# A transformer block on one core: group A's y kept whole, the last pair projected by halves, a third buffer for probability pieces, and a root on GpSimd

## The chip, the cores and the metric

The kernel runs on one core of one Trainium2 chip, in float32 throughout its interface. The metric is device time in microseconds (us), the median of several runs; lower is better. The engines are called by these names: TensorE (PE in the profile, PEld for its weight loads), VectorE (DVE), ScalarE (ACT), GpSimd (POOL) and SyncE (SP), whose queue issues nearly all DMAs of this kernel.

## The reference

A block of a streaming encoder for 1024 tokens of width 1024, cut to what matters:

```python
n = rms_norm(x, norm1_g)
proj = n @ w_in                       # columns: qa 512, ka 128, va 128, qb 512, kb 512, vb 512
ya = mixer_a(qa, ka, va, sinks)       # 8 heads of 64, 2 key heads, window of 3 chunks of 64, ALiBi, sinks
yb = mixer_b(qb, kb, vb, rel_bias)    # 8 heads of 64, own chunk and 8 before it, a bias by clipped distance
y = concat(rms_norm(ya, out_norm_a_g), rms_norm(yb, out_norm_b_g))
h = x + y @ w_out
u = square(relu(rms_norm(h, norm2_g) @ w_ff1))   # 1024 -> 4096
h = h + u @ w_ff2                                # 4096 -> 1024
out = rms_norm(h, final_norm_g)
```

## The kernel before, in words

**Precision.** A float32 operand is split into a high part (rounded, written by ScalarE) and a low part (what is left, by VectorE or GpSimd), and a product is three matmuls, high x high, high x low and low x high (`mm3`, L193). So every operand of a product costs one ScalarE copy and one subtraction before TensorE may read it.

**Stages.** First the input is loaded, normalised and split into `nT[t][hl][g]` (L257): two halves of 512 tokens, high and low, four tiles each, 16 pages in all. A *page* (L94) is a tile of 4 KB for each partition; 35 of them (`NPAGES`) serve in turn for weights, projected q, k and v, y and the rest. Weights come through three *stages* (L97): `load_weight` (L209) loads 512 KB into a stage, and makes the high part on ScalarE (L223) and the low part on GpSimd in pieces of 256 columns (L228). Then group A's attention runs, then group B's, then the output projection and the two feed-forward products, which are TensorE from end to end.

**Attention.** Heads go in pairs, four of group A and four of group B. A unit of group B (`UnitB`, L754) is one head and one half of the queries, so a pair has four units. For each block of 128 queries it computes scores on TensorE, adds the bias and takes the minimum on VectorE (L570, L572), and the exponential on ScalarE (L573). `upper` (ScalarE, L805) and `lower` (VectorE, L810) turn two blocks of probabilities into float16 high and low pieces H (tag `P16`, two buffers), and a transposing DMA on SyncE's queue (L813) brings H to G, which the matmul `av` reads (`apply`, L823). The bias of one head lies in one of two tiles `bias_b`; it is loaded in two DMAs (L613, L614) that leave out two corners, which were set to a large negative value once (L532, L533). The bias of the next user of a tile is asked for at score 1 of the unit before (`next_bias`, L786).

**What fills TensorE meanwhile.** A queue of generators, the `Filler` (L901), is worked off in steps between the rows of attention: 16 steps, of three matmuls each, for every projection of k, q or v of a later pair (`in_proj`, L433), and at the end 64 steps of group A's share of the output projection, `op_A` (`out_proj_a`, L954). `ready(2)` (L911) runs the first piece of the first two generators of the queue, up to their first `yield`: that piece asks for weights, and for "out" it loads group A's y for the first 512 tokens (L888) and four output weights. So "out" is begun when the last v projection comes to the head of the queue.

```python
    def step(self):
        while self.queue:
            self.ready(2)
            try:
                next(self.queue[0][1])
                return
            except StopIteration:
                self.queue.pop(0)
```

TensorE's order is the program's, written out by hand (`pe`, L130). The other engines' and SyncE's orders are set by a scheduler when the kernel is built, from its own estimate of times; each engine then works strictly in that order, and so a waiting instruction holds up what is queued behind it.

**Group A's y.** When both heads of a pair have done a half of the tokens, `finish` (L625) squares Y for the group's norm (GpSimd, L659, L669, L670), splits Y into a page y by `split_y` (L850) and stores it, 512 KB, to `yd` in DRAM (L638). For pairs 0 and 1 the split applies the gain `ogc` (L854 on ScalarE, L857 on VectorE); pairs 2 and 3 (`PLAIN`) are split without a gain (L860 on ScalarE, two subtractions on GpSimd), and the gain is applied to the output weight instead, by an extra ScalarE pass over each half of the stage (L222). The norm's factor `rA` comes from `group_rstd` (L867): eight matmuls, and then an inverse root by four Newton steps of four small VectorE instructions (L878 to L881). It is read first where `op_A` is moved out of PSUM (L976). Group B's last pair keeps its y on the chip, in two pages `y7` named ahead (L989).

Of the kernel before, what the change touches and what calls it, by code (L numbers as in the profile page):

```python
# [17 lines left out]
P = 128  # L18
SEQ = 1024
D = 1024  # L20
# [10 lines left out]
WITH = ["", "", "k", "qv", "k", "qv", "k", "qv"]  # L31
NPAGES = 35
LOW_COLS = 256
# [10 lines left out]
POOL_NORM = ((1, 0), (1, 1))  # L44
PLAIN = (2, 3)
EARLY = 7
# [6 lines left out]
def kernel(  # L53
# [37 lines left out]
    def f(ap):  # L91
        return ap.bitcast(F32)
# [115 lines left out]

    def load_weight(src, shape, name, low_engine, cuts=1, pieces=1, gain=None):  # L209

        st = stage(shape, f"st_{name}")
        w = [page(shape, f"w{hl}_{name}") for hl in range(2)]
        key = "o" if name[0] == "o" else None

        def steps():
            n = shape[1] // cuts
            for i in range(0, shape[1], n):
                load(st[:, i : i + n], src[:, i : i + n])
                for j in range(i, i + n, n // pieces):
                    c = slice(j, j + n // pieces)  # L220
                    if gain is not None:
                        in_turn(key, nc.scalar.activation(st[:, c], st[:, c], AF.Copy, scale=gain))  # L222
                    in_turn(key, nc.scalar.activation(w[0][:, c], st[:, c], AF.Copy))  # L223
# [15 lines left out]

    yd = dram([8, P, 2, 2, HALF], "yd")  # L240
    hB = [dram([P, 2, D], f"hB{n}") for n in range(TB // 2)]
# [147 lines left out]
    def values_b(acc, name, dst, t):  # L389

        if t == 0:
            halves[name] = main.tile([P, 2, HALF], F32, tag="tst", bufs=2, name=f"ts_{name}")
        st = halves[name]
# [38 lines left out]

    def in_proj(c0, kind, name, dst, new):  # L433

        w = proj_weight(c0, name, nc.gpsimd)
        yield
        for t in range(2):
            acc = aps.tile([P, HALF], F32, tag="w", bufs=2, name=f"ip_{name}_{t}")
            for k in range(NK):
                project(acc, w, t, (k,))  # L440
                if k == NK - 1:
                    if t == 0 and new is not None:
                        dst.extend(new(name))
                    place(acc, kind, name, dst, t, nc.gpsimd)
                yield

    dve, pool = nc.vector, nc.gpsimd
# [82 lines left out]
    bias_b = [at.tile([P, 5 * P], F32, name=f"b_B{s}") for s in range(2)]  # L530
    for b in bias_b:
        nc.gpsimd.memset(b[:HD, 5 * P - HD :], NEG)  # L532
        nc.gpsimd.memset(b[HD:, :HD], NEG)  # L533

# [52 lines left out]
    class Pair:  # L587
# [7 lines left out]
        def biases(self):  # L595
            if self.kind == "A" and self.j == 0:
                return first_bias
            if self.bias:
                return self.bias
            for s in range(2):  # L600
                if self.kind == "B":
                    self.load_bias(s)
                    continue
                h = 2 * self.j + s
                b = atA.tile([P, 2 * P], F32, tag="bias", bufs=2, name=f"b_A{h}")
                nc.sync.dma_start(b, dist)
                nc.gpsimd.tensor_scalar(b, b, 2.0 ** -(h + 1), None, ALU.mult)
                self.bias.append(b)
            return self.bias

        def load_bias(self, s):
            b = bias_b[s]
            nc.sync.dma_start(b[:HD, : 5 * P - HD], relb[2 * self.j + s][:HD, : 5 * P - HD])  # L613
            nc.sync.dma_start(b[HD:, HD:], relb[2 * self.j + s][HD:, HD:])  # L614
# [7 lines left out]
        def gain(self):  # L622
            return self.V[2] if self.kind == "B" else None

        def finish(self, t):  # L625

            by_act = self.kind == "B" and self.m < 7
            if not by_act:
                self.squares(t, by_act)
            Y = self.out[t]  # L630
            if self.y is None:
                y = page([P, 2, HALF], f"y{t}_{self.m}")
                low = split_y(y, Y, self.m, by_act, self.gain())

                def rest():
                    if by_act:
                        low()
                    nc.sync.dma_start(yd[self.m, :, t], f(y))  # L638

                if by_act:  # L640
                    late.append(rest)
                else:
                    rest()
            else:
                split_y(self.y[t], Y, self.m, False, self.gain())
            if by_act:
                self.squares(t, by_act)
# [106 lines left out]
    class UnitB:  # L754
# [10 lines left out]
        def score(self, b):  # L765
# [20 lines left out]
        def next_bias(self):  # L786
# [3 lines left out]
            pairs_b[j].load_bias(s)  # L790

# [57 lines left out]

    def split_y(y, src, m, wait=False, gain=None):  # L850

        if m not in PLAIN:
            gain = ogc[:, m : m + 1] if gain is None else gain
            nc.scalar.activation(y[:, 0], src, AF.Copy, scale=gain)  # L854

            def low():
                return nc.vector.scalar_tensor_tensor(y[:, 1], src, gain, f(y[:, 0]), ALU.mult, ALU.subtract)  # L857

            return low if wait else low()
        nc.scalar.activation(y[:, 0], src, AF.Copy)  # L860
        for c in (slice(c, c + LOW_COLS) for c in range(0, HALF, LOW_COLS)):
            split_l(nc.gpsimd, y[:, 1, c], src[:, c], y[:, 0, c])

    def new_y(m):
        return [page([P, 2, HALF], f"y{t}_{m}") for t in range(2)]

    def group_rstd(kind, psum, tag, bufs, r):  # L867
# [9 lines left out]
        for _ in range(4):  # L877
            nc.vector.tensor_tensor(q, r, r, ALU.mult)  # L878
            nc.vector.tensor_tensor(q, q, v, ALU.mult)
            nc.vector.tensor_scalar(q, q, -0.5, 1.5, ALU.mult, ALU.add)  # L880
            nc.vector.tensor_tensor(r, r, q, ALU.mult)  # L881
        return r

    nc.vector.tensor_scalar(nsink, psink, -1.0, None, ALU.mult)
    def load_y(m, halves=range(2)):
        y = [page([P, 2, HALF], f"y{t}_{m}") for t in halves]
        for tile_y, t in zip(y, halves):
            nc.sync.dma_start(f(tile_y), yd[m, :, t])  # L888
        return y

    def out_weight(m):

        return load_weight(w_out[m * P : (m + 1) * P, :], [P, D], f"o{m}", pool, 1, 2, ogc[:, m : m + 1] if m in PLAIN else None)

# [6 lines left out]
    class Filler:  # L901
# [79 lines left out]
    fill = Filler()  # L981
    units = []
    fill.add("A1", ahead_A1, True)
    for j in range(4):
# [3 lines left out]
        units += [(UnitA(pair, i0), f"A{j}", A_FILL) for i0 in range(0, TB, 2)]  # L988
    y7 = new_y(7)  # L989
    for j in range(4):  # L990
        Q, K, V = [], [], []
        fill.add(f"B{j}", in_proj(KB0 + j * P, "k", f"kB{j}", K, new_k))
        fill.add(f"B{j}", in_proj(QB0 + j * P, "q", f"qB{j}", Q, new_q))
        fill.add(f"B{j}", in_proj(VB0 + j * P, "v", f"vB{j}", V, None))
        pair = Pair("B", j, Q, K, V, y7 if j == 3 else None)
# [598 lines left out]
```

## Time and profile before

| | |
|---|---|
| median of 3 runs | 1059.55 us (1058.63 to 1060.02) |
| the profiled execution | 1060.42 us |
| its span, first to last instruction | 1058.6 us |
| granted TensorE clock, mean of the span | 0.988 |
| busy: TensorE, VectorE, ScalarE, GpSimd | 1024.1, 690.4, 585.1, 420.7 us |
| group A's y: stores and loads of group A and B | 14 and 14, 512 KB each |
| DMA traffic | 187.71 MB, mean 177 GB/s |

In a line of the profile, "L165 PE MATMUL op_A<-w_o,y" is a matmul issued at line 165 (a helper) that writes tile op_A and reads w_o and y; buffer numbers are left out. In the timeline the first two columns are the start and the duration in us, and a bracket gives the idle time of the engine before the instruction and what released it. SPq is the issuing of DMAs by SyncE: its duration is that of the issue, not of the transfer. In the table of stretches each engine has its busy time and, in brackets, its count of instructions; PEclk is the share of the full clock that was granted to TensorE. In a group of instructions, three durations stand for the shortest, the median and the longest in ns.

### The profile page before, as it was taken

To read this page: it belongs to the slowest core of one execution; us is meant where nothing else is said; L and a number is where in the kernel's file an instruction comes from. 1 tells how busy PE (TensorE), PEld (TensorE's weight loads), DVE (VectorE), ACT (ScalarE), POOL (GpSimd) and SP (SyncE) were. 2 spreads that over 40 slices of the span, in tenths; PEclk is the share of its full clock that TensorE was granted. 3 is DMA by queue.
4 is the path that set the end of the run, shared out by engine and by line. 5 is a ranking of instruction groups with operands and counts; after the bars stand their busy time and mean duration, and the time that the engine had idled before them with its cause. 6 is when DMAs were issued, how large, how long until landed. Compare 5 with 4: busy or idle time off the path is not lost.

```text
span 1058.6 us, 13930 instructions
## 1 busy us (share of the span) xinstructions
PE 1024.1 (97%) x4803; PEld 832.7 (79%) x4803; DVE 690.4 (65%) x1075; ACT 585.1 (55%) x973; POOL 420.7 (40%) x307
## 2 busy tenths in 40 slices
PE   9999999979968899999999999999999999999997
PEld 7888887757746768888888888888888888888886
DVE  6577787858654725796434425436879877778667
ACT  8677767647664756675554454455533333333347
POOL 0566785322343373305554444345114024024025
PEclk9999999989989999999999999999999999999999
DMA  9954548899899993315534525417997535532004
GB/s 356 264 151 132 144 111 205 177 206 212 178 253 247 208 310 117 119 47 177 193 122 163 191 104 179 159 74 246 379 400 252 179 122 164 179 114 98 1 1 159
DMA packets 145222, 187.71 MB, mean 177 GB/s; under 512 B 78848, under 2 KB 96256, under 8 KB 145152
## 3 DMA queue, kind: packets, MB, share of 16 engines
q1 hardware_dynamic: 145008, 186.56, 58.4%
q8 instruction: 38, 0.62, 0.2%
q14 instruction: 32, 0.26, 0.1%
q10 hardware_dynamic: 144, 0.26, 0.1%
HBM read 105.00 MB, written 45.09 MB: 142 GB/s over the span
## 4 chain that ended last, share of the span: by engine, by line
PE 61%; DVE 2%; DMA 1%; ACT 1%; issue 0%; ACTq 0%; DVEq 0%
PE f L165 27%; PE f_a L165 16%; PE f_c L165 8%; PE op_B L165 4%; PE f_b L165 4%; DMA G_B<-H_B 1%; DVE X L171 1%; PE tp L168 0%; PE end L165 0%; PE op_A L165 0%; DVE S L1139 0%; DVE T L1168 0%; PE ss_B L165 0%; DVE H_B L810 0%; PE av_B L165 0%
## 5 line engine op out<-in xcount | busy, mean ns | idle before, releaser
L165 PE MATMUL f<-X,W 128*128 128x512 f32 x1344 | 305.9, 389 | 0.1
L165 PEld LDWEIGHTS f<-X,W 128*128 128x128 f32 x1344 | 252.0, 188 | 52.9 <-DVE X L171 0.5
L165 PE MATMUL f_a<-V,U 128*128 128x512 f32 x756 | 173.5, 389 | 0.0
L171 POOL TENSOR_TENSOR U<-u,U 128x1024 fp32r<-128x1024 f32 x32 | 79.7, 2492 | 227.5 <-PE f_c L165 135.8
L165 PEld LDWEIGHTS f_a<-V,U 128*128 128x128 f32 x756 | 141.8, 188 | 29.7 <-DVE C L1483 0.3
L171 POOL TENSOR_TENSOR W<-T,W 128x1024 fp32r<-128x1024 f32 x29 | 75.7, 2612 | 139.3 <-ACT W L1190 139.3
L165 PE MATMUL f_c<-V,U 128*128 128x512 f32 x384 | 88.4, 389 | 0.0
L165 PEld LDWEIGHTS f_c<-V,U 128*128 128x128 f32 x384 | 72.1, 188 | 15.0
L1190 ACT ACTIVATE V<-Z 128x1024 fp32r<-128x1024 f32 x32 | 33.9, 1059 | 88.3 <-PE f_a L165 44.6
L810 DVE SCALAR_TENSOR_TENSOR H_B<-P_B,rc_B,H_B 128x640 f16<-128x640 f32 (+2 forms) x64 | 52.8, 847 | 31.6 <-ACT H_B L805 31.3
L171 POOL TENSOR_TENSOR W<-w,W 128x1024 fp32r<-128x1024 f32 x23 | 57.2, 2490 | 32.1 <-ACT W L1190 32.0
L1190 ACT ACTIVATE V<-w 128x1024 fp32r<-128x1024 f32 x24 | 25.4, 1059 | 80.1 <-issue 34.3
L1239 DVE TENSOR_TENSOR k<-f,k 128x1024 f32<-128x1024 f32 x24 | 29.3, 1221 | 61.9 <-PE f L165 61.9
L171 DVE TENSOR_TENSOR V<-w,V 128x1024 fp32r<-128x1024 f32 x24 | 50.4, 2103 | 27.2 <-ACT V L1190 26.8
L573 ACT ACTIVATE P_B<-P_B,nm_B 128x640 f32<-128x640 f32 (+2 forms) x64 | 44.3, 692 | 42.7 <-DVE nm_B L570 22.0
L165 PE MATMUL op_A<-w_o,y 128*128 128x512 f32 x192 | 56.7, 426 | 8.7 <-ACT w_o L223 6.8
L1190 ACT ACTIVATE U<-u 128x1024 fp32r<-128x1024 f32 x56 | 58.5, 1045 | 11.4 <-DMA ud<-k 6.8
L165 PE MATMUL av_B<-G_B,VvB 128*128 128x128 f16 (+3 forms) x208 | 44.6, 302 | 13.5 <-DMA G_B<-H_B 13.5
L1233 ACT ACTIVATE k<-f 128x1024 f32<-128x1024 f32 x24 | 24.6, 1026 | 59.2 <-PE f L165 59.2
L805 ACT ACTIVATE H_B<-P_B,rc_B 128x640 f16<-128x640 f32 (+2 forms) x64 | 40.9, 686 | 22.8 <-DMA G_B<-H_B 12.1
L165 PE MATMUL ip_qB<-nT,w_qB 128*128 128x512 f32 x192 | 52.0, 405 | 1.1 <-DVE ts_kB L359 0.8
L165 PE MATMUL ip_kB<-nT,w_kB 128*128 128x512 f32 x192 | 52.6, 401 | 0.0
(245 smaller groups left out, 1934.5 us busy)
## 6 DMA issues: line engine op xcount, KB each, us to landing
w<-in_w_ff_dram SPq DMA_DIRECT2D x64, 512.0 KB, 4.9
u<-ud SPq DMA_DIRECT2D x56, 512.0 KB, 4.6
ud<-k SPq DMA_DIRECT2D x48, 512.0 KB, 3.2
KkB<-ts_kB SPq DMA_DIRECT2D x64, 128.0 KB, 2.3
yd<-y SPq DMA_DIRECT2D x14, 512.0 KB, 3.1
y<-yd SPq DMA_DIRECT2D x14, 512.0 KB, 7.3
xr<-in_x_dram SPq DMA_DIRECT2D x8, 512.0 KB, 8.7
QqB<-ts_qB SPq DMA_DIRECT2D x32, 128.0 KB, 2.9
```

The costliest lines, as they stand in the source:

```text
L165: pe(nc.tensor.matmul(*args, **kw))
L171: return engine.tensor_tensor(lo, full, f(hi), ALU.subtract)
L573: nc.scalar.activation(pr, pr, AF.Exp, bias=nm, scale=-1.0, accum_out=sm)
L805: nc.scalar.activation(hi, q, AF.Copy, scale=rc)
L810: nc.vector.scalar_tensor_tensor(lo, q, rc, hi, ALU.mult, ALU.subtract)
L1190: nc.scalar.activation(w[0], full, AF.Copy)
L1233: nc.scalar.activation(kept[p], ps, AF.Copy)
L1239: dve.tensor_tensor(v, ps, v, ALU.add)
```

## The change

Five edits go together.

1. *Group A's y is stored unsplit.* `finish` stores Y itself, 256 KB, to a new array `ya`. `load_ya` loads it into the low half of a page and splits it there with the gain, for all four pairs; `PLAIN` and the ScalarE pass over the weights are gone. In `out_proj_a` each weight is now asked for ahead of its y.
2. *The last pair of group B is projected by halves.* Its q and v projections run as one generator: both for the first 512 tokens, then both for the second. Both weights are asked for at its start. "out" is no longer begun as the second of the queue, but by `fill.start("out")` after the first halves. The staging tile of this v is a page, and the two pages `y7` are no longer named ahead.
3. *A third buffer* for H (`P16`), with 34 pages and not 35.
4. *The Newton steps* of group A's root run on GpSimd.
5. *The bias of group B* is loaded whole, in one DMA, and its two corners are set by two memsets on GpSimd after each load, at score 3 of the unit before its use (at once for the first pair).

```diff
-NPAGES = 35
+NPAGES = 34
-PLAIN = (2, 3)
...
-                    if gain is not None:
-                        in_turn(key, nc.scalar.activation(st[:, c], st[:, c], AF.Copy, scale=gain))
...
-    yd = dram([8, P, 2, 2, HALF], "yd")
+    yd = dram([3, P, 2, 2, HALF], "yd")
+    ya = dram([4, P, 2, HALF], "ya")
...
+            if name == "vB3":
+                halves[name] = page([P, 2, HALF], f"ts_{name}", F32)
+            else:
+                halves[name] = main.tile([P, 2, HALF], F32, tag="tst", bufs=2, name=f"ts_{name}")
...
+    def in_proj_halves(q, v):
+
+        w = [proj_weight(a[0], a[2], nc.gpsimd) for a in (q, v)]
+        yield
+        for t in range(2):
+            for a, wa in zip((q, v), w):
+                yield from in_proj(*a, wa, (t,))
+            if t == 0:
+                fill.start("out")
...
         def load_bias(self, s):
-            b = bias_b[s]
-            nc.sync.dma_start(b[:HD, : 5 * P - HD], relb[2 * self.j + s][:HD, : 5 * P - HD])
-            nc.sync.dma_start(b[HD:, HD:], relb[2 * self.j + s][HD:, HD:])
-            self.bias.append(b)
+            nc.sync.dma_start(bias_b[s], relb[2 * self.j + s])
+            self.bias.append(bias_b[s])
+
+        def mask_bias(self, s):
+            nc.gpsimd.memset(bias_b[s][:HD, 5 * P - HD :], NEG)
+            nc.gpsimd.memset(bias_b[s][HD:, :HD], NEG)
...
             Y = self.out[t]
-            if self.y is None:
+            if self.kind == "A":
+                nc.sync.dma_start(ya[self.m, :, t], Y)
+            elif self.y is None:
...
-            if b == 1:
-                self.next_bias()
             if b % 2:
-                H = at.tile([P, 20 * P], F16, tag="P16", bufs=2, name=f"H_{self.name}_{b}")
+                self.next_bias(b == 1)
+            if b % 2:
+                H = at.tile([P, 20 * P], F16, tag="P16", bufs=3, name=f"H_{self.name}_{b}")
...
+    def split_y(y, src, gain, wait=False):
+
+        nc.scalar.activation(y[:, 0], src, AF.Copy, scale=gain)
+
+        def low():
+            return nc.vector.scalar_tensor_tensor(y[:, 1], src, gain, f(y[:, 0]), ALU.mult, ALU.subtract)
+
+        return low if wait else low()
...
         for _ in range(4):
-            nc.vector.tensor_tensor(q, r, r, ALU.mult)
-            nc.vector.tensor_tensor(q, q, v, ALU.mult)
-            nc.vector.tensor_scalar(q, q, -0.5, 1.5, ALU.mult, ALU.add)
-            nc.vector.tensor_tensor(r, r, q, ALU.mult)
+            nc.gpsimd.tensor_tensor(q, r, r, ALU.mult)
+            nc.gpsimd.tensor_tensor(q, q, v, ALU.mult)
+            nc.gpsimd.tensor_scalar(q, q, -0.5, 1.5, ALU.mult, ALU.add)
+            nc.gpsimd.tensor_tensor(r, r, q, ALU.mult)
...
+    def load_ya(m, t):
+        y = page([P, 2, HALF], f"y{t}_{m}")
+        nc.sync.dma_start(f(y[:, 1]), ya[m, :, t])
+        split_y(y, f(y[:, 1]), ogc[:, m : m + 1])
+        return y
...
         def ready(self, n):
             for item in self.queue[:n]:
-                if not item[2]:
+                if not item[2] and (item[0] != "out" or item is self.queue[0]):
+                    next(item[1])
+                    item[2] = True
+
+        def start(self, name):
+            for item in self.queue:
+                if item[0] == name and not item[2]:
                     next(item[1])
                     item[2] = True
...
         for m in range(4):
-            ys.append(load_y(m, (0,)))
-        for m in range(4):
             ws.append(out_weight(m))
+            ys.append([load_ya(m, 0)])
         yield
         for tb in range(TB):
             if tb == 1:
                 for m in range(4):
-                    ys[m] += load_y(m, (1,))
+                    ys[m].append(load_ya(m, 1))
...
-    y7 = new_y(7)
...
+        q, v = (QB0 + j * P, "q", f"qB{j}", Q, new_q), (VB0 + j * P, "v", f"vB{j}", V, None)
+        if j < 3:
+            fill.add(f"B{j}", in_proj(*q))
+            fill.add(f"B{j}", in_proj(*v))
+        else:
+            fill.add(f"B{j}", in_proj_halves(q, v))
```

More of the change, by code (lines that the diff above doesn't have):

```diff
@@ L207, in in_turn, with load_weight @@
             last_act[key] = ins.ins.name
-    def load_weight(src, shape, name, low_engine, cuts=1, pieces=1, gain=None):
+    def load_weight(src, shape, name, low_engine, cuts=1, pieces=1):
         st = stage(shape, f"st_{name}")
@@ L431, in new_v, with in_proj @@
         return [page([P, 4, 2, 2 * HD], f"V{name}{t}") for t in range(2)]
[L433 to L437, printed above, removed]
+    def in_proj(c0, kind, name, dst, new, w=None, ts=range(2)):
+        if w is None:
+            w = proj_weight(c0, name, nc.gpsimd)
+            yield
+        for t in ts:
             acc = aps.tile([P, HALF], F32, tag="w", bufs=2, name=f"ip_{name}_{t}")
@@ L530 @@
     bias_b = [at.tile([P, 5 * P], F32, name=f"b_B{s}") for s in range(2)]
-    for b in bias_b:
-        nc.gpsimd.memset(b[:HD, 5 * P - HD :], NEG)
-        nc.gpsimd.memset(b[HD:, :HD], NEG)
     rows_of_a = [0]
@@ L602, in biases @@
                     self.load_bias(s)
+                    self.mask_bias(s)
                     continue
@@ L620, in rows @@
             return self.out[t]
-        def gain(self):
-            return self.V[2] if self.kind == "B" else None
         def finish(self, t):
@@ L630, in finish @@
             Y = self.out[t]
-            if self.y is None:
+            if self.kind == "A":
+                nc.sync.dma_start(ya[self.m, :, t], Y)
+            elif self.y is None:
                 y = page([P, 2, HALF], f"y{t}_{self.m}")
-                low = split_y(y, Y, self.m, by_act, self.gain())
+                low = split_y(y, Y, self.V[2], by_act)
                 def rest():
@@ L637, in rest @@
                         low()
-                    nc.sync.dma_start(yd[self.m, :, t], f(y))
+                    nc.sync.dma_start(yd[self.m - 4, :, t], f(y))
                 if by_act:
@@ L644, in finish @@
             else:
-                split_y(self.y[t], Y, self.m, False, self.gain())
+                self.y.append(page([P, 2, HALF], f"y{t}_{self.m}"))
+                split_y(self.y[t], Y, self.V[2])
             if by_act:
@@ L778, in score, with next_bias @@
             self.P[b] = exponentials("B", self.i0 + b, p.biases()[self.s], BIG, S, pt, self.nm[:, c], self.sm[:, c])
-            if b == 1:
-                self.next_bias()
             if b % 2:
-                H = at.tile([P, 20 * P], F16, tag="P16", bufs=2, name=f"H_{self.name}_{b}")
+                self.next_bias(b == 1)
+            if b % 2:
+                H = at.tile([P, 20 * P], F16, tag="P16", bufs=3, name=f"H_{self.name}_{b}")
                 defer.append((self, lambda: self.upper(b - 1, H)))
                 defer.append((self, lambda: self.lower(b - 1, H)))
-        def next_bias(self):
+        def next_bias(self, load):
             s, j = 1 - self.s, self.pair.j + self.s
@@ L789, in next_bias @@
                 return
-            pairs_b[j].load_bias(s)
+            if load:
+                pairs_b[j].load_bias(s)
+            else:
+                pairs_b[j].mask_bias(s)
         def pieces(self, b, H):
@@ L848, in apply @@
                 p.finish(self.t)
[L850 to L865, printed above, removed]
+    def split_y(y, src, gain, wait=False):
[3 more added lines that the diff above has]
+        return low if wait else low()
     def group_rstd(kind, psum, tag, bufs, r):
@@ L887, in load_y @@
         for tile_y, t in zip(y, halves):
-            nc.sync.dma_start(f(tile_y), yd[m, :, t])
+            nc.sync.dma_start(f(tile_y), yd[m - 4, :, t])
+        return y
[3 more added lines that the diff above has]
+        split_y(y, f(y[:, 1]), ogc[:, m : m + 1])
         return y
     def out_weight(m):
-        return load_weight(w_out[m * P : (m + 1) * P, :], [P, D], f"o{m}", pool, 1, 2, ogc[:, m : m + 1] if m in PLAIN else None)
+        return load_weight(w_out[m * P : (m + 1) * P, :], [P, D], f"o{m}", pool, 1, 2)
     hres = {}
@@ L981 @@
     fill = Filler()
-    units = []
+    units, y7 = [], []
     fill.add("A1", ahead_A1, True)
```

5 lines of the change are left out of this document (2 added, 3 removed).

## The prediction

> **What bounds the kernel now.** I read the head of the page first, then TensorE's busy time and clock by stretches, then the waits of TensorE, and last the timeline around the longest of them.
>
> ```profile
> span 1058.6 us, 13930 instructions
> ## 1 busy us (share of the span) xinstructions
> PE 1024.1 (97%) x4803; PEld 832.7 (79%) x4803; DVE 690.4 (65%) x1075; ACT 585.1 (55%) x973; POOL 420.7 (40%) x307
> ```
>
> TensorE is the bound, and the change alters no matmul. It can save only TensorE's idle time, 1058.6 - 1024.1 = 34.5 us, and the time that TensorE runs at a reduced clock. The next rows (stretch, busy time of PE, PEld, DVE, ACT and POOL, granted clock, DMA share, GB/s) show where both lie.
>
> ```profile
> 210.00:220.00 10.00, 6.53 (x32) 4.35 (x32) 5.72 (x17) 4.92 (x11) 2.39 (x3) 1.00 0.84 171
> 220.00:230.00 10.00, 7.15 (x41) 5.50 (x39) 5.26 (x19) 4.67 (x10) 3.44 (x5) 0.86 0.92 195
> 230.00:240.00 10.00, 9.71 (x43) 7.90 (x42) 6.06 (x21) 5.27 (x10) 0.00 (x0) 0.80 0.96 239
> 300.00:310.00 10.00, 6.39 (x31) 4.40 (x29) 6.80 (x14) 3.61 (x8) 4.44 (x6) 0.96 1.02 281
> 310.00:320.00 10.00, 4.95 (x11) 2.53 (x12) 3.59 (x6) 9.06 (x15) 6.10 (x7) 0.50 1.10 238
> 320.00:330.00 10.00, 10.00 (x45) 6.81 (x45) 4.71 (x14) 5.43 (x14) 2.06 (x2) 0.86 0.85 207
> 340.00:350.00 10.00, 4.33 (x17) 3.32 (x17) 6.40 (x10) 6.41 (x13) 6.78 (x5) 0.83 1.04 317
> sum 70.00, PE 49.06 PEld 34.81 DVE 38.55 ACT 39.37 POOL 25.22; mean PE 7.01 PEld 4.97 DVE 5.51 ACT 5.62 POOL 3.60
> ```
>
> These seven stretches, all in group B's attention, hold 70.00 - 49.06 = 20.9 of the 34.5 us. I count busy time x (1 - clock) as lost to the clock. Three places follow. **Place 1** (300 to 330, the start of group A's output projection): idle 3.61 + 5.05 = 8.7, clock 0.26 + 2.48 + 1.40 = 4.1, together 12.8 us. **Place 2** (340 to 350): idle 5.7, clock 0.7, together 6.4. **Place 3** (210 to 240): idle 6.6, clock 1.0 + 1.9 = 2.9, together 9.5. That is 28.7 us in all, the most that the change can reasonably aim at. The waits say what ends them (engine, matmul, releaser: sum, times, longest):
>
> ```profile
> PE av_B L165 <- DMA G_B<-H_B: 13.5, 6, 5.3
> PE op_A L165 <- ACT w_o L223: 6.8, 2, 4.6
> PE pt_A L168 <- DVE T_A L171: 1.5, 1, 1.5
> PE op_A L165 <- POOL w_o L171: 1.4, 2, 0.7
> ```
>
> Place 1 is the two op_A rows, 8.2 us: the output weights come late. Places 2 and 3 are av_B, waiting for the DMA that transposes probability pieces (H to G).
>
> **Place 1: the loads of the output projection.** SyncE's queue, TensorE, and the first scaling pass on ScalarE (start, duration, what; idle time before it in brackets):
>
> ```profile
> 298.65 1.98 SPq L888 DMA_DIRECT2D y<-yd  x4
> 300.68 0.73 SPq L121 DMA_DIRECT2D st_o<-in_w_out_dram  x1
> 301.51 8.68 SPq L813 DMA_TRANSPOSE G_B<-H_B  x1
> 310.30 0.52 SPq L121 DMA_DIRECT2D st_o<-in_w_out_dram  x1
> ```
> ```profile
> 311.42 0.80 PE L165 MATMUL op_A<-w_o,y 128*128 128x512 f32 x1 [4.62 <-ACT w_o L223]
> 312.92 1.22 PE L165 MATMUL op_A<-w_o,y 128*128 128x512 f32 x2 [0.70 <-POOL w_o L171]
> 316.36 0.79 PE L165 MATMUL op_A<-w_o,y 128*128 128x512 f32 x1 [2.22 <-ACT w_o L223]
> ```
> ```profile
> 309.99 0.72 ACT L222 ACTIVATE st_o<-st_o,ogc 128x512 f32<-128x512 f32 x1 [5.17 <-DMA st_o<-in_w_out_dram]
> ```
> ```profile
> y<-yd SPq DMA_DIRECT2D x14, 512.0 KB, 7.3
> ```
>
> Four y of 512 KB and the third weight (a load of the same size: 128x1024 floats), 2.6 MB, are issued from 298.65; the weight lands at 309.99. That is 11.3 us, about 230 GB/s. The transpose stands behind them on the same queue, takes 8.68 us to issue, and holds the fourth weight back to 310.30. The change reads y as unsplit halves of 256 KB, 1.05 MB less, an estimated 4.5 us at that rate; places each weight ahead of its y; and drops the scaling passes, four of 0.72 us. TensorE wanted the third weight at 311.42 - 4.62 = 306.8. It comes 4.5 + 0.7 = 5.2 us sooner, so that wait is gone. The fourth comes at 316.36 - 4.5 - 1.4 = 310.5 where TensorE, after its three matmuls (0.8 + 1.2 us at the low clock), wants it at about 307.8: 2.7 left, and about 0.6 for its low half, 3.3 us idle. For the clock I leave 1.5. So by traffic and passes alone the place falls from 12.8 to 4.8: **-8.0**.
>
> The other lever is memory. In the code "out" is begun at the first step of the last v projection, 16 steps from that projection's end; `start("out")` also falls 16 steps from the end. The moment in the program is thus the same. What differs is that q and v of the first 512 tokens are both done by then, so the eight pages of nT[0] are free at once and not eight steps later. If pages were the limit, the whole 12.8 goes. The ends are 0 (the earlier loads only push back transposes) and 12.8; I keep 8.0, because it needs only the rows above.
>
> On the way back y costs eight splits:
>
> ```profile
> L854 ACT ACTIVATE y<-Y,ogc x4: 707/712/717, 67.5 to 117.4; 128x512 fp32r<-128x512 f32 x4
> L857 DVE SCALAR_TENSOR_TENSOR y<-Y,ogc,y x4: 739/1238/1672, 68.3 to 118.7; 128x512 fp32r<-128x512 f32 x4
> L860 ACT ACTIVATE y<-Y x4: 621/628/634, 127.5 to 180.4; 128x512 fp32r<-128x512 f32 x4
> L171 POOL TENSOR_TENSOR y<-Y,y x8: 737/744/751, 131.6 to 182.1; 128x256 fp32r<-128x256 f32 x8
> ```
>
> ScalarE: 8 x 0.71 = 5.7 us in the projection, of which the first four (2.8) replace the four passes (2.9); net nothing ahead of op_A. VectorE: 8 x 0.74 to 1.67 us, 3.0 to 6.7 before op_A; it is busy 6.80 and 3.59 of 10 us there, so there is room. Were it gone, the price is those 3.0 us. In group A the splits leave: four of VectorE, eight of ScalarE, eight of GpSimd. TensorE waits there hardly at all; the row that I can tie to it is pt_A, 1.5 us, and I take **-0.5** (ends 0 and -1.5). That Y is now held until its store has landed is covered by its second buffer: the next half of a pair writes the other one.
>
> **Place 2: the third buffer.**
>
> ```profile
> 337.46 8.39 SPq L813 DMA_TRANSPOSE G_B<-H_B  x2
> ```
> ```profile
> 341.87 0.80 ACT L805 ACTIVATE H_B<-P_B,rc_B 128x128 f16<-128x128 f32 x2 [6.52 <-DMA G_B<-H_B]
> ```
> ```profile
> 341.81 0.22 PE L165 MATMUL av_B<-G_B,VvB 128*128 128x128 f16 x1 [0.40 <-DMA G_B<-H_B]
> 347.30 0.91 PE L165 MATMUL av_B<-G_B,VvB 128*128 128x384 f16 x3 [5.28 <-DMA G_B<-H_B]
> ```
> ```profile
> 220.90 5.02 SPq L371 DMA_DIRECT2D KkB<-ts_kB  x8
> 226.02 3.54 SPq L813 DMA_TRANSPOSE G_B<-H_B  x2
> ```
> ```profile
> 230.29 0.90 PE L165 MATMUL av_B<-G_B,VvB 128*128 128x384 f16 x3 [2.05 <-DMA G_B<-H_B]
> ```
>
> ScalarE stands 6.52 us before it may write the next H, because both buffers are in transposes; the second of the two transposes needs that H, and TensorE waits 5.28 us for it. With a third buffer H is ready early, and two transposes in a row may take 3.54 us as at 226.02 and not 8.39: 4.8 us sooner, at best all of 6.4. At worst nothing: loads ahead of them slow them, whoever fills H. I take **-3.5**, a little over half.
>
> **Place 3** is different: at 220.90 SyncE spends 5.02 us on eight copies before it issues the transposes at 226.02, and a third buffer doesn't move that. Two edits relieve the place slightly:
>
> ```profile
> L614 SPq DMA_DIRECT2D b_B<-in_relb_dram x8: 477/587/1763, 49.8 to 326.9; - x8
> L532 POOL MEMSET b_B<- x2: 145/146/146, 37.6 to 37.9; 64x64 f32 x2
> ```
> ```profile
> L976 ACT ACTIVATE o<-op_A,rgA x16: 665/687/693, 320.1 to 388.7; 128x512 f32<-128x512 f32 x16
> L878 DVE TENSOR_TENSOR qgA<-rgA x4: 161/167/168, 228.5 to 233.1; 128x8 f32<-128x8 f32 x4
> ```
>
> A bias is loaded by one DMA and not two, 0.59 us of SyncE each time, and the root's 16 small steps, 16 x 0.167 = 2.7 us, leave VectorE. I take **-1.5** of the 9.5 (ends 0 and -5). On GpSimd a step costs between 0.146 (a memset) and 0.744 us (a subtraction of 256 columns), nearest to the first since it has 8 columns: 2.3 to 11.9 us in series. It starts at about 228.5 and is first read at 320.1, so 90 us of other work hide it; uncovered it would be up to 11.9.
>
> **What is added.** Each bias is now masked by two memsets after its load: 0.3 us on GpSimd, and VectorE's scores wait for it. Behind the memset on GpSimd wait the low halves of weights. No row shows this wait; it is 0 if GpSimd is free, 4 x 0.74 + 0.3 = 3.3 us if it stands behind a weight. Six handovers (pairs 1 to 3) matter; I take 0.25 us each, nearer to the low end since the load is asked for two scores ahead of the mask: **+1.5**. The last v projection begins eight steps earlier than now, so its weight must be split earlier: 0 to 3.0 us (four subtractions), taken as **+1.0**.
>
> **Sum**: -8.0 - 3.5 - 1.5 - 0.5 + 1.5 + 1.0 = -11.0 us. The profiled execution took 1060.42 us (its span and 1.8 around it), so 1049.4; the median of the runs is 0.9 lower, 1059.55, so 1048.5.
>
> The clock is the softest part of it. In 210 to 220 TensorE is idle for 3.5 us and the clock stays at 1.00; in the next 10 us it is idle for 2.9 and the clock falls to 0.86. The Trainium skill ("TensorE: Matmul & The Clock Gate", Part 1) says that the clock halves only after an idle window of about 3.4 us, and that the window runs freely. By that rule the 3.3 us that I leave at place 1 would cost no clock, and the sum would be 1.5 us lower, 1047.0; the rows just named show that shorter pauses do cost, so I keep the 1.5.
>
> **Rivals.** *Larger gain*: pages were the limit, and the first two places vanish: -12.8 - 6.4 - 4.5 (half of place 3) + 1.0 = -22.7, 1036.9. For it: nT[0] is free 16 steps ahead of the projections' end and not eight. Against it: the transpose of 8.68 us shows DMA as the limit. Chance 0.08.
>
> *Given back*: loads that start earlier meet the transposes of the units running then, and av_B waits take over 6 of the 8.0; places 2 and 3 give 1 between them, additions cost 2.5. Sum -0.5, about 1059. For it: DMA share is 1.02 to 1.10 in 300 to 320 already. Against it: fewer bytes in all. Chance 0.12.
>
> *Slower*: the mask. If each of the six handovers waits the full 3.3 us on GpSimd, and the scores, H and transposes behind them pass it on to TensorE, that is +19.8 against -13.5 + 1.0: +7.3, 1066.9. It decides from 12.5 / 6 = 2.1 us per handover. For it: av_B already waits six times, so this chain has no slack there. Against it: GpSimd is busy under half of the time in these stretches, and no row of TensorE's waits names a bank that holds scores. Chance 0.15.
>
> **Numbers.** The forecast, 1048.5, has 0.65, with its own range 1041 to 1056. A change of 0.2%, 2.1 us, is about what can be told from none. Faster: 0.65 + 0.08 + 0.04 of the given-back case = 0.77; same 0.07; slower 0.15 + 0.01 = 0.16. The range 1040 to 1062 takes in the forecast and the given-back case and leaves out most of the larger gain and of the slower case.
>
> **What would show it.** Right: op_A waits for w_o below 4 us in sum with a clock near 1 after its start; ScalarE's H no longer waiting for the DMA of G; av_B's waits down to about 8 us from 13.5; the root's steps on GpSimd with nobody waiting. Wrong: memsets of the bias with waits before them and VectorE's scores waiting for GpSimd; transposes of over 8 us while the output loads run and av_B waits grown; a wait of the last v projection for its weight.

## The result, and the profile after

The kernel after took 1062.87 us (median of 11 runs, 1061.54 to 1066.37) against 1060.02 us before (11 runs, 1058.15 to 1061.20): the ratio is 1.0033, 95% interval 1.0021 to 1.0045. It is slower by 0.3%, where 1.0% faster was predicted (1048.5 against 1059.55). The profiled execution took 1062.87 us, its span 1061.1.

The head of the page of the kernel after, in the order of before:

```profile
span 1061.1 us, 13980 instructions
## 1 busy us (share of the span) xinstructions
PE 1027.7 (97%) x4803; PEld 834.4 (79%) x4803; DVE 702.1 (66%) x1063; ACT 582.6 (55%) x969; POOL 424.3 (40%) x327
```

The same 4803 matmuls. TensorE's idle time fell only from 34.5 to 33.4 us, and its busy time for them grew by 3.6 us; the granted clock, as a mean of the span, is 0.986 where it was 0.988. The stretches of the kernel after:

```profile
200.00:210.00 10.00, 8.48 (x39) 5.50 (x39) 7.99 (x23) 6.72 (x15) 1.49 (x4) 1.00 0.82 189
210.00:220.00 10.00, 8.79 (x45) 5.96 (x44) 6.30 (x16) 5.75 (x13) 4.40 (x5) 1.00 0.82 168
220.00:230.00 10.00, 6.93 (x41) 5.23 (x41) 6.28 (x16) 5.91 (x12) 4.35 (x7) 0.93 0.94 189
230.00:240.00 10.00, 9.41 (x39) 7.43 (x39) 2.83 (x9) 3.21 (x6) 2.87 (x15) 0.73 0.88 249
300.00:310.00 10.00, 7.31 (x36) 5.38 (x34) 7.73 (x13) 9.41 (x19) 8.12 (x10) 1.00 1.03 270
310.00:320.00 10.00, 6.76 (x17) 3.94 (x18) 9.18 (x19) 6.62 (x12) 4.89 (x9) 0.53 1.08 264
320.00:330.00 10.00, 10.00 (x50) 7.18 (x48) 4.86 (x16) 5.00 (x12) 0.00 (x0) 0.96 0.88 215
330.00:340.00 10.00, 6.60 (x22) 4.29 (x21) 6.03 (x11) 5.21 (x10) 4.52 (x4) 0.72 1.14 274
340.00:350.00 10.00, 10.00 (x50) 7.26 (x50) 5.21 (x11) 6.65 (x13) 5.26 (x4) 0.94 0.77 253
380.00:390.00 10.00, 5.54 (x19) 3.41 (x17) 0.00 (x0) 1.72 (x3) 6.45 (x8) 0.83 1.06 311
```

and three stretches of the kernel before that the prediction does not show:

```profile
200.00:210.00 10.00, 10.00 (x52) 7.00 (x51) 8.77 (x23) 8.09 (x18) 4.61 (x5) 1.00 0.78 179
330.00:340.00 10.00, 10.00 (x51) 6.95 (x50) 3.67 (x11) 2.82 (x7) 2.54 (x2) 1.00 1.07 273
380.00:390.00 10.00, 8.77 (x45) 5.77 (x44) 0.68 (x1) 5.33 (x9) 8.99 (x12) 1.00 1.04 308
```

Counted as in the prediction (idle time, and busy time x (1 - clock)), **place 1** went from 12.8 to 9.5 us and **place 2** from 6.4 to 0.6. But two places are new: 330 to 340, from 0 to 5.2 us, and 380 to 390, from 1.2 to 5.4. The waits of TensorE after:

```profile
PE av_B L164 <- DMA G_B<-H_B: 10.5, 5, 4.5
PE op_A L164 <- ACT o L994: 3.4, 1, 3.4
PE op_A L164 <- ACT y L867: 2.4, 1, 2.4
PE op_A L164 <- DVE y L870: 2.2, 1, 2.2
PE pt_A L167 <- DVE T_A L170: 2.0, 1, 2.0
PE op_A L164 <- DVE up_vB L403: 1.4, 1, 1.4
PE S_B L164 <- DVE nm_B L579: 1.1, 1, 1.1
```

The waits for w_o are gone, as predicted; waits for the split of y (L867, L870) and for the eviction o have come in their place, and one wait for the transposes is still 4.5 us long. The two kernels run the same matmuls and, but for those of the last q and v projections, in the same order, so their starts can be subtracted one by one. A score matmul of group B at 296.83 us started 1.60 later in the kernel after; an op_A at 325.49 started 1.81 **earlier**, those from 354.95 to 382.03 2.72 earlier; the first op_B, at 389.42, started 2.28 later, and every matmul after that by 2.2 to 2.5. So the kernel after gained 4.3 us between 297 and 355 us, and lost 5.0 us in one place right at the end of attention. Here is that place on SyncE's queue, after and then before:

```profile
371.06 1.02 SPq L984 DMA_DIRECT2D h<-in_x_dram  x2
372.17 1.93 SPq L895 DMA_DIRECT2D y<-yd  x4
375.25 7.73 SPq L828 DMA_TRANSPOSE G_B<-H_B  x1
```
```profile
372.29 1.05 SPq L966 DMA_DIRECT2D h<-in_x_dram  x2
373.40 0.90 SPq L888 DMA_DIRECT2D y<-yd  x2
375.23 6.42 SPq L813 DMA_TRANSPOSE G_B<-H_B  x1
```

and TensorE at the matmuls that read that transpose, after and before:

```profile
385.10 0.48 PE L164 MATMUL av_B<-G_B,VvB 128*128 128x384 f16 x2 [4.46 <-DMA G_B<-H_B]
385.29 1.45 PE L164 MATMUL op_A<-w_o,y 128*128 128x512 f32 x3
```
```profile
384.42 0.48 PE L165 MATMUL av_B<-G_B,VvB 128*128 128x384 f16 x2 [1.07 <-DMA G_B<-H_B]
384.61 0.99 PE L165 MATMUL op_A<-w_o,y 128*128 128x512 f32 x3
```

The last transpose of attention is issued at the same moment in both, 375.2 us, although TensorE is 2.7 us ahead. Its input H, from the last softmax, is ready no earlier: VectorE begins the low half of it 1.4 us sooner, but the same two instructions take 1.4 us longer (after, then before):

```profile
372.11 3.11 DVE L825 SCALAR_TENSOR_TENSOR H_B<-P_B,rc_B,H_B 128x640 f16<-128x640 f32 x2
```
```profile
373.54 1.67 DVE L810 SCALAR_TENSOR_TENSOR H_B<-P_B,rc_B,H_B 128x640 f16<-128x640 f32 x2
```

Four loads of y (512 KB each, group B's, read only from op_B on) now stand ahead of it where two stood, it takes 7.73 in place of 6.42 us to issue, and TensorE waits 4.46 us, after which it runs at a lower clock at first (three matmuls take 1.45 us in place of 0.99). Of the 5.0 us, 2.7 are the lead that is waited away, 0.7 the later start of av_B (385.10 against 384.42), and 1.6 the slower run from there to the first op_B.

The stall at 335 us begins with a load too: h of the first 128 tokens, asked for when "out" makes its first step, stands on SyncE's queue behind the transposes of v. In the kernel after, three engines, one row each:

```profile
328.91 0.52 SPq L984 DMA_DIRECT2D h<-in_x_dram  x1
```
```profile
332.59 2.53 POOL L995 TENSOR_TENSOR h<-h,o 128x512 f32<-128x512 f32 x2 [13.05 <-DMA h<-in_x_dram]
```
```profile
335.46 2.93 PE L164 MATMUL op_A<-w_o,y 128*128 128x512 f32 x6 [3.40 <-ACT o L994]
```

In the kernel before the same load went out at 325.85. The evictions o (op_A moved out of PSUM by ScalarE) have two buffers; GpSimd frees them by adding them to h, and it stands idle for 13 us until h lands. TensorE, now early, fills both and stands until the third can be evicted.

### The profile page after: what moved, and what is told of

It is laid out like the page before. It is cut to its first block, busy times and chain, and to the rows that moved or that the text cites. A ratio compares the mean times of both kernels' runs of the same rounds, so it can differ in the third digit from the quotient of the medians.

```text
span 1061.1 us, 13980 instructions
## 1 busy us (share of the span) xinstructions
PE 1027.7 (97%) x4803; PEld 834.4 (79%) x4803; DVE 702.1 (66%) x1063; ACT 582.6 (55%) x969; POOL 424.3 (40%) x327
## 4 chain that ended last, share of the span: by engine, by line
PE 56%; DVE 1%; ACT 0%; issue 0%; ACTq 0%
PE f L164 27%; PE f_a L164 16%; PE f_c L164 8%; PE f_b L164 4%; PE end L164 0%; DVE X L170 0%; DVE T L1189 0%; DVE k L1260 0%; ACT fo L145 0%; DVE S L1153 0%; DVE S L1160 0%; ACT uf L145 0%; DVE wf L145 0%; ACT C L145 0%; DVE S L1152 0%
## 5 line engine op out<-in xcount | busy, mean ns | idle before, releaser
L1211 ACT ACTIVATE V<-Z 128x1024 fp32r<-128x1024 f32 x32 | 33.9, 1060 | 90.9 <-PE f_a L164 44.6
L1211 ACT ACTIVATE V<-w 128x1024 fp32r<-128x1024 f32 x24 | 25.4, 1059 | 78.8 <-issue 34.2
L164 PE MATMUL op_A<-w_o,y 128*128 128x512 f32 x192 | 59.0, 441 | 9.3 <-ACT o L994 3.4
L170 DVE TENSOR_TENSOR V<-w,V 128x1024 fp32r<-128x1024 f32 x24 | 45.4, 1891 | 27.3 <-ACT V L1211 24.3
L164 PEld LDWEIGHTS op_A<-w_o,y 128*128 128x128 f32 x192 | 38.0, 208 | 18.4 <-DVE y L870 4.7
L1211 ACT ACTIVATE W<-w 128x1024 fp32r<-128x1024 f32 x24 | 25.3, 1058 | 47.4 <-PE f L164 23.0
```

The source lines that it names most:

```text
L164: pe(nc.tensor.matmul(*args, **kw))
L170: return engine.tensor_tensor(lo, full, f(hi), ALU.subtract)
L1211: nc.scalar.activation(w[0], full, AF.Copy)
```

## The experiments

**Theory A**: the end of attention is set by the chain last softmax, H, last transpose, and by the loads ahead of that transpose on its queue; what TensorE gains earlier is waited away there. **Theory B**, the rival: there is no such single point, and the result is the sum of small new waits (h and o, y splits, masks) that ate the gains. The kernel before, timed beside the experiments, took 1060.3 to 1060.6 us. Differences between experiments are of medians; taken from the ratios to the kernel before they come out up to 1.1 us different, so the figures are good to about 1 us. A trace is of one run, and not always of a typical one.

**e1_y_behind: the kernel after, with group B's six y loads behind the last transpose.** A dependency without a semaphore keeps SyncE's order:

```diff
-            nc.sync.dma_start(f(tile_y), yd[m - 4, :, t])
+            ins = nc.sync.dma_start(f(tile_y), yd[m - 4, :, t])
+            if behind:
+                tc.add_manual_dep(ins.ins, behind, dep, reason="program order")
...
         while defer and not nexts:
             defer.pop(0)[1]()
+        if unit is units[-1][0]:
+            ys += [[], [], []]
+            for t in range(2):
+                for m in (4, 5, 6):
+                    ys[m - 4] += load_y(m, (t,), last_turn[0])
```

> The changed kernel, with the loads of group B's six y halves put behind the last transpose of probability pieces on SyncE's queue (and in the order first halves, then second). Theory A (the end of attention is set by the last transpose, which stands behind four y loads of 512 KB; what TensorE gained earlier, 2.7 us at 378 us, is spent waiting there, and the wait lowers the clock): the av_B wait near 381 us falls from 4.46 to under 1 us, op_B begins 4 us earlier than 391.7, and the time is 1058 to 1059.5 us. Theory B (the loss is the sum of small new waits, mask, scores, splits, all before 340 us): the end of attention moves by under 1 us and the time stays at 1062 to 1064.

Measured: 1057.83 us, ratio to before 0.9982 (0.9972 to 0.9992): 5.0 us less than the kernel after, from the place and order of six loads alone, and just below theory A's range; theory B's is missed by 4 us. SyncE's queue at the place:

```profile
372.80 1.02 SPq L987 DMA_DIRECT2D h<-in_x_dram  x2
377.00 3.06 SPq L828 DMA_TRANSPOSE G_B<-H_B  x1
380.15 2.74 SPq L895 DMA_DIRECT2D y<-yd  x5
```

The transpose takes 3.06 us, and TensorE no longer waits for it. What follows: a main term of the loss is this place. (The profiled run, 1059.77, is among the slowest of its twelve.)

**e2_h_early: the kernel after, with h of the first 128 tokens loaded together with the output loads.**

```diff
             ys.append([load_ya(m, 0)])
+        h = hres[0] = page([P, D], "h0", F32)
+        nc.sync.dma_start(h, x[:P, :])
         yield
```

> The changed kernel, with the load of the first residual tile h asked for when the output projection's loads are, and not at its first step. It aims at the 3.4 us for which op_A waits at 335 us for the copy o, whose two buffers wait for GpSimd's additions and these for h. Theory A: that wait goes, TensorE runs about 5 us ahead of the changed kernel by 375 us, and waits all of it at the last transpose: 8 to 9 us there, time 1061.5 to 1064, no gain. Theory B: the time falls by the wait and its clock, 4 to 6 us, to 1057 to 1059.

Measured: 1058.57 us, 0.9989 (0.9977 to 1.0000), 4.3 us less than the kernel after. The 3.4 us wait for o is gone. Theory A in its strict form fell here: it expected no gain while the y loads stay in front. Theory B's range, 1057 to 1059, held. In the profiled run, the slowest of the twelve (1061.14; the others go down to 1056.05), the last transpose still takes 7.76 us behind four y loads, but it is issued at 373.76 in place of 375.25: TensorE was 4.2 us ahead of before at 366 us, and the last scores, and so their H, came earlier. TensorE still loses 5.0 us there (first op_B 0.8 later than before), and had lost 4.8 before that, of a lead of 9.0 us at 350 us, around a wait of 3.23 us for another transpose at 354. So TensorE's progress does feed the chain, with a part of its lead only.

**e3_both: both mends.**

> Both edits, y behind the last transpose and h early. Theory A: together they give what neither gives alone: 1053 to 1057 us. Theory B: the second gives its 4 to 6 us and the first nothing: 1057 to 1059.

Measured: 1053.53 us, 0.9941 (0.9928 to 0.9953), 9.3 us below the kernel after, the sum of the two alone (5.0 + 4.3), and faster than both kernels. Theory A's range held. But each mend also gives its part alone, where each theory expected nothing of one of them: the time was lost at two places. The first op_B starts at 382.36, 7.1 earlier than before, and the span is shorter by the same 7.1 (1051.5 against 1058.6). What holds TensorE up there is now an eviction:

```profile
382.36 8.48 PE L164 MATMUL op_B<-w_o,y 128*128 128x512 f32 x36 [1.40 <-ACT o L1001]
```

**e4_y_behind_on_before: the same six loads behind the last transpose, in the kernel before** (the edit of e1).

> The kernel before, with the same six loads behind its last transpose. There TensorE waits 1.07 us for that transpose, behind two y loads. Theory A: the wait goes, 1058 to 1059.5 us. Theory B says nothing of the kernel before: within 0.5 us of it.

Measured: 1059.68 us, 0.9992 (0.9983 to 1.0000): 0.7 us, between the two expectations and hardly to be told from none. The transpose takes 3.08 us here too, but TensorE waited only 1.07 us for it in the kernel before, so there was little to get. So the order of these loads matters much more in the kernel after, where TensorE comes early and four of them stand in front.

**e5_buf2 and e7_both_buf2: two buffers for H again**, in the kernel after and in the one with both mends.

```diff
-                H = at.tile([P, 20 * P], F16, tag="P16", bufs=3, name=f"H_{self.name}_{b}")
+                H = at.tile([P, 20 * P], F16, tag="P16", bufs=2, name=f"H_{self.name}_{b}")
```

> The kernel after with two buffers for pieces again (the pool of pages stays at 34), nothing else changed. Before: 1060.3, after: 1062.9. Theory A (the end of attention is set by the last transpose, its H and the loads ahead of it on SyncE's queue; in the kernel after TensorE arrives there 2.7 us earlier than before and waits 4.46 us): H_B waits for G_B again, TensorE loses the 3 to 4 us at 340 to 350 us, but that is taken out of its wait at the last transpose: 1062 to 1064.5, and the last wait av_B<-G_B shrinks below 3 us. Theory B (what TensorE gains or loses on the way reaches the end): the third buffer is worth the 3.5 us of the prediction, so 1066 to 1067.5.

> The kernel with both mends (group B's y loads behind the last transpose, the load of h0 with the output loads; 1053.5) and two buffers for pieces in place of three. Theory A: with the end of attention clear, TensorE and the softmax chain both count, and the third buffer's part shows: 1056 to 1058, by the 3.5 us of the prediction or somewhat less. If the third buffer is worth nothing: 1053 to 1054.

Measured: 1063.12 us (1.0019, 1.0009 to 1.0030; the kernel after has 1.0033) and 1055.20 us (0.9954, 0.9941 to 0.9968, against 0.9941). In the kernel after the third buffer is worth nothing that can be told from none; with the end mended the medians differ by 1.7 us, between the two expectations, but the intervals overlap: a gain of the third buffer is not shown. In e5 TensorE was 1.3 us ahead of before at 380 us and waited 4.8 us at the last transpose. But that wait did not shrink, as theory A had said it would: the transpose was issued later as well, at 376.62. The two traces also show what became of place 2 without the third buffer, e5 and then e7:

```profile
340.00:350.00 10.00, 10.00 (x47) 7.26 (x46) 5.92 (x14) 6.08 (x13) 5.76 (x5) 0.86 1.07 268
```
```profile
340.00:350.00 10.00, 10.00 (x55) 8.18 (x54) 8.20 (x17) 8.03 (x17) 5.55 (x4) 1.00 1.02 320
```

TensorE does not stand still there with two buffers either.

**e6_no_halves and e8_both_no_halves: q, then v, whole, and output loads begun as in the kernel before**, in the kernel after and in the one with both mends.

```diff
-                if not item[2] and (item[0] != "out" or item is self.queue[0]):
+                if not item[2]:
...
-        if j < 3:
+        if True:
             fill.add(f"B{j}", in_proj(*q))
             fill.add(f"B{j}", in_proj(*v))
```

> The kernel after with q and v of the last pair projected whole, one after the other, and output loads begun where the kernel before begins them (as second in the queue of work to fill in); the rest of the change stays. Theory A: TensorE is later by up to 3.5 us at 325 us (in the kernel after it gained that between 298 and 325 us), has 2.7 us of slack before the last transpose, and the h load that TensorE waits for at 335 us may move: 1062 to 1065. Theory B: the prediction's place 1 is worth 8 us, and without it the time is 1067 to 1071. If the unsplit y with its splits on return is what makes place 1 wait, the wait there stays on y and the time is near 1063 whatever the halves do.

> The kernel with both mends and the last pair projected whole, output loads begun where the kernel before begins them. By the prediction's place 1 (8 us): 1060 to 1062. By what the two traces show between 298 and 325 us (3.4 us): 1056 to 1058. If the wait at place 1 is bound by the y splits on return: 1053 to 1054.

Measured: 1060.86 us (1.0004, 0.9995 to 1.0013), 2.0 **less** than the kernel after, below all its expectations (1062 to 1065, 1067 to 1071, near 1063); and 1060.37 us (0.9997, 0.9985 to 1.0010), 6.8 **more** than with halves, as expected from the prediction's 8 us (1060 to 1062). The same edit has opposite signs on the two sides. TensorE in e6 stands still for one long wait at the start of op_A, because the last v projection now ends just before it:

```profile
316.05 1.62 PE L164 MATMUL op_A<-w_o,y 128*128 128x512 f32 x3 [11.81 <-DVE ts_vB L395]
335.32 1.66 PE L164 MATMUL op_A<-w_o,y 128*128 128x512 f32 x6 [0.16 <-ACT o L994]
```

The second row is the stall on h and o: with op_A later, h is there in time, and 0.16 us is left of 3.40. TensorE is then 5.5 us ahead of before at 350 us, more than in the kernel after, and arrives too early at the last transpose, which takes 7.92 us behind four y loads. With both mends, then, the halves and the begin of the output loads that goes with them are worth 6.8 us; in the kernel after, the place of h's load and of the y loads hides them. Not all of the 6.8 lies at place 1: in the trace of e8 (1062.86, its slowest run) op_A waits 13.26 us at its start, and 3.53 more at 340 us for an eviction o, which on ScalarE comes behind splits that wait for the next y loads:

```profile
335.65 1.99 ACT L867 ACTIVATE y<-y,ogc 128x512 fp32r<-128x512 f32 x3 [4.59 <-DMA y<-ya]
```

**e9_both_mask: both mends, and group B's bias in two loads, masked once**, as before.

```diff
-            nc.sync.dma_start(bias_b[s], relb[2 * self.j + s])
+            nc.sync.dma_start(b[:HD, : 5 * P - HD], relb[2 * self.j + s][:HD, : 5 * P - HD])
+            nc.sync.dma_start(b[HD:, HD:], relb[2 * self.j + s][HD:, HD:])
```

> The kernel with both mends (1053.5), with the bias of group B loaded in two parts and masked once at the start, as in the kernel before. By the prediction the memsets after each load cost 1.5 us and the second DMA of a load 0.6 us of SyncE each: without the one and with the other 1052 to 1053. If the memsets hold the scores up (the slower rival): 1047 or less. If they are hidden: 1053.5 to 1055.

Measured: 1056.39 us, 0.9963 (0.9951 to 0.9976), 2.9 more than with one load and memsets (the intervals just touch). None of the three expectations had that size. In the trace the loss comes at 354 us, where TensorE waits for the first transpose of the last units:

```profile
354.13 0.69 PE L164 MATMUL av_B<-G_B,VvB 128*128 128x384 f16 x3 [4.20 <-DMA G_B<-H_B]
```

In e3 that wait is 1.71. The transpose, issued at 345.38 and 345.20, takes 5.57 in place of 3.74 us; three loads of output weights and three of h go out in the 8 us before it in e9, one and three in e3. Why one more small DMA at 305 and one at 317 us shift that was not settled.

**e10_both_newton_dve: both mends, the root's steps on VectorE.**

```diff
-            nc.gpsimd.tensor_tensor(q, r, r, ALU.mult)
+            nc.vector.tensor_tensor(q, r, r, ALU.mult)
```

(and its three companions likewise)

> The kernel with both mends, the root's steps on VectorE as in the kernel before. By the prediction a part of its 1.5 us at place 3 (16 steps of 0.167 us that leave VectorE): up to 1.5 us slower, 1054 to 1055. If the root is hidden on either engine: 1053 to 1054.

Measured: 1053.71 us, 0.9937 (0.9924 to 0.9951): no difference from e3. The root's engine costs and saves nothing that can be told from none.

**e11_both_ya_split: both mends, group A's y split before it is stored**, and loaded as 512 KB a half.

```diff
-                nc.sync.dma_start(ya[self.m, :, t], Y)
+                y = page([P, 2, HALF], f"y{t}_{self.m}")
+                split_y(y, Y, ogc[:, self.m : self.m + 1])
+                nc.sync.dma_start(ya[self.m, :, t], f(y))
```

> The kernel with both mends, with group A's y split before it is stored, stored and loaded as two parts of 512 KB a half, and not split on return; weights, halves and the early begin stay. By the prediction's traffic term (1.05 MB in the first half at 230 GB/s, 4.5 us): 1057 to 1059. If the splits on return (op_A waits of 1.2, 2.5 and 1.4 us at 308 to 316 us) cost what the bytes save: 1052 to 1054.

Measured: 1056.46 us, 0.9965 (0.9952 to 0.9978), 2.9 more than with the unsplit y: between the two expectations. At place 1 itself this version is ahead (its op_A at 325.49 of before starts 4.9 us earlier, in e3 1.7); it loses that from 328 us on, where transposes behind the larger loads take 10.12 us for two:

```profile
328.49 1.82 SPq L905 DMA_DIRECT2D y<-ya  x4
330.36 0.42 SPq L991 DMA_DIRECT2D h<-in_x_dram  x1
330.88 10.12 SPq L830 DMA_TRANSPOSE G_B<-H_B  x2
```

In e3 the same two take 6.25. So in these two traces the smaller loads pay through the transposes, not through place 1. As with e9, the intervals of e11 and e3 just touch.

**e12_both_ya_earlier: both mends, the y loads asked for in pairs behind the first two weights.**

```diff
         for m in range(4):
             ws.append(out_weight(m))
-            ys.append([load_ya(m, 0)])
+            if m < 2:
+                ys += [[load_ya(n, 0)] for n in (2 * m, 2 * m + 1)]
```

> The kernel with both mends; the loads of unsplit y are asked for in pairs, the first two behind the first weight, the other two behind the second, so that fewer of them stand behind the transpose of 5.6 us at 299 us. If place 1 is bound by the late loads of y (issued 304.5 to 307.3 us, behind that transpose): op_A's waits on y (3.7 us) go below 2 and the time is 1050.5 to 1052.5. If the weights that now come later take their place: 1053 to 1055.

Measured: 1058.30 us, 0.9979 (0.9970 to 0.9987), 4.8 more than e3, worse than either expectation. SyncE:

```profile
296.45 1.01 SPq L903 DMA_DIRECT2D y<-ya  x2
297.51 2.13 SPq L120 DMA_DIRECT2D st_o<-in_w_out_dram  x3
299.74 7.08 SPq L828 DMA_TRANSPOSE G_B<-H_B  x1
```

One more load ahead of the transpose at 299 us, and it takes 7.08 in place of 5.63 us, which holds back the loads behind it. op_A's wait for y grew from 1.22 to 3.45 us, and a transpose wait of 3.88 us followed at 355.

## Why the prediction was wrong

**The sum was the step that failed.** "-8.0 - 3.5 - 1.5 - 0.5 + 1.5 + 1.0 = -11.0" takes every saving at a stall of TensorE as one at the end. Nothing in the working asked what TensorE waits for next when a stall goes, and what sets the end of attention. It was in the profile of before: its last transpose took 6.42 us behind loads and TensorE waited for it already, if only 1.07 us. TensorE came 2.7 us early there and left 2.3 us late. Mending that place gives 5.0 us (e1), mending the new stall on h 4.3 (e2), and both 9.3 (e3). Even then the kernel is 6.3 us faster than before (0.9941), not 11.0, so terms of the sum were mis-sized too.

**Place 1, -8.0.** Measured at the place, -3.3. The weights did come early. What came late in their stead:

```profile
308.94 0.73 PE L164 MATMUL op_A<-w_o,y 128*128 128x512 f32 x2 [2.36 <-ACT y L867]
311.84 0.79 PE L164 MATMUL op_A<-w_o,y 128*128 128x512 f32 x1 [2.17 <-DVE y L870]
315.34 2.08 PE L164 MATMUL op_A<-w_o,y 128*128 128x512 f32 x4 [1.40 <-DVE up_vB L403]
```

"VectorE is busy 6.80 and 3.59 of 10 us there, so there is room" was read from the kernel before. The change itself fills that room: with the halves the last v's evictions, its row maxima and the split of a y of group B fall into the same 10 us, and VectorE is 9.18 us busy in 310 to 320. The alternative price that the prediction named, 3.0 us, is near the 2.17 + 1.40 that TensorE waited for VectorE. Three of the four y loads also stood behind a transpose, issued from 304.80 on, which the working, by bytes alone, did not have. With the mends the halves give 6.8 (e8) and the unsplit y 2.9 (e11) at the end; that these are near 8.0 is in part luck, for both include time lost at other places, and the two were not taken out together.

**Place 2, -3.5.** The first half of the mechanism was right: ScalarE's H no longer waits for G (12.1 us of such waits before, none after), H at that point comes at 332.57 and not 341.87, and 340 to 350 went from 6.4 to 0.6. The second half, that this frees TensorE, was not: in e5, with two buffers, ScalarE waits 10.2 us for G again, that H comes at 340.61, and no matmul waits for it; e7 has no stall there either. So the third buffer is not needed for it: another part of the change closes the place. It is not the halves alone, for in e6, without them, TensorE is 10.00 us busy in 340 to 350 too; which part it is stays open. And the prediction did not say what is late next: that was h, behind the transposes of v, 5.2 us at 330 to 340, which e2 removes.

**Place 3, -1.5.** 210 to 240 went from 9.5 to 7.9 us, the number that was predicted, and 200 to 210 lost 1.5 by a new wait of scores for VectorE, so the net is nothing. The wait stands in e9 and e10 as well, with the mask and the root as before; its cause stays open. The root part is zero within the noise (e10), so the matching number does not confirm the reasoning.

**Group A, -0.5.** Not seen: at 176 us the kernel after is 0.4 us later, and profiled runs of the kernels above, which run group A alike, differ there by 2 us.

**The mask, +1.5, and the slower rival on it.** The sign is wrong for the edit as a whole: undoing it costs 2.9 (e9), by a shift of loads whose cause is not settled. The memsets do wait for their loads, 30.7 us in all, but no wait of TensorE names what is queued behind them on GpSimd; the row of op_A for POOL's w_o, 1.4 us before, is gone.

**The last v weight earlier, +1.0.** Between 286 and 293 us the lag grows from 1.0 to 1.6 us, but 0.42 of that is a wait for a transpose, at 292.94, and no wait of TensorE names the weight.

**The rivals.** The direction was that of "given back": loads meet transposes. But that case had it at the first output loads and at 0.12, and it ended at no change. The real one was later loads of another group, which the change did not touch. The result, 1062.87, lies outside the range of 1040 to 1062.

**The clock.** The 1.5 us left for it at place 1 were 3.6. The Trainium skill ("TensorE: Matmul & The Clock Gate", Part 1) has an idle window of about 3.4 us as what halves the clock. Read as "shorter pauses cost none", this does not hold here: the longest pause at place 1 is 2.36 us, and the clock in 310 to 320 is 0.53, so the measurement decides against that reading. What the traces show is pauses that add up. The granted clock is one half for 3.41 us or a multiple of it, in the kernel after for 10.24 us from 310.5 on, and in the 3.41 us before that TensorE was idle for 2.68 us in pieces. In all fourteen traces, between the start-up and the end of the program, each such stretch began after at least 2.0 us of idle time within 3.41 us, and no 3.41 us with less idle time cost the clock, but for one drop at 227 to 231 us that follows 0.7 to 2.3 us of it and stays unexplained.

## What to carry to other kernels

Before adding up savings at stalls, find the chain that ends the stage, and ask of each saving whether it makes that chain earlier; an engine that comes early to a fixed point only waits longer. Look at what stands ahead of a transfer that somebody waits for, and put loads with later users behind it: six loads moved gave 5.0 us here, and only after another change had made them matter. Undo a part on both sides of such a block, because its sign may turn: the halves cost 2.0 us with the block and gave 6.8 without it. And test the edit itself before it gets the credit for a stall that went: place 2 closed, but not through the third buffer.

## What the runs showed of the hardware

The same transpose of a 128x2560 H, last of attention, takes to issue 3.00 to 3.09 us with no y load ahead of it (e1, e3, e4, e7, e8, e10, e11, e12; 3.50 in e9), 6.42 with two loads of 512 KB (before), 7.73, 7.76, 7.92 and 8.05 with four (after, e2, e6, e5). The first two loads cost 3.4 us, the next two 1.3 to 1.6.

A small step of the root takes 0.20 us on GpSimd against 0.17 on VectorE. The low half of the last H on VectorE took 3.11 us in the kernel after and 1.67 before, with GpSimd busy 9.61 and 8.20 us of the 10 us around. In e1, e2 and e3 it took 3.09 to 3.11 too; no run took that apart.
